# One layer of a hybrid encoder: the pieces of the folded down-projection weights move from SyncE's queue to ScalarE's, and their subtractions are tied to VectorE's order

## The chip, the cores and the metric

The kernel runs on 1 core of one Trainium2 chip. The metric is the device time of one execution in microseconds (us). Three executions of the kernel before took 2810.12, 2808.11 and 2813.13 us (median 2810.12).

## What is computed

One layer is applied to a prompt of 2048 rows and to 8 short sequences of 16 rows, all of width 1024:

```python
h = rms_norm(x, norm_g[0])
z = h @ w_in                      # columns split among attention heads and memory heads
att = band_attention(...)         # 8 heads x 64, own chunk and 8 chunks before, relative bias
mem = mlstm_sequence(...)         # 4 heads x 128, a recurrent matrix memory
x = x + rms_norm(concat(rms_norm(att), sigmoid(o) * head_norm(mem)) @ w_out, norm_g[1])
u = rms_norm(x, norm_g[2]) @ w_up # 1024 x 5632
y = causal_conv_width_3(u); gate, up = split(y)
x = x + rms_norm((gelu(gate) * up) @ w_down, norm_g[3])   # w_down: 2816 x 1024
```

Keys, values, memory states and convolution tails are outputs too.

## The kernel before

All matmuls run in fp32 pieces: each operand is split into a high part (a ScalarE cast or copy) and a low part (a VectorE subtraction), and `mm3` (L99 to L103) issues three matmuls per product.

The program has two large stages. In the first, rows are normed and multiplied by `w_in` in 14 column groups for each half of the rows (`seq`, 28 groups in all). While TensorE does those projections, two streams are interleaved with them by `pump`: band attention (lines 334 to 450) and the matrix memory (lines 500 to 800). The output projection by `w_out` follows. In the second stage, `w_up`, the convolution and `w_down` run in three row blocks. For the first two blocks, the products are done by a scheme of seven multiplications instead of eight, which needs sums and differences of blocks of the weights.

The differences of `w_down` are made ahead of time, in the first stage, by `folds` (L1163 to L1190). A row group of `w_down` holds four 128 x 512 blocks; `folds` handles 11 row groups in two halves each, 22 pieces. For a piece:

- `load` fetches 512 KB, 128 partitions by 4 by 256 numbers, into a buffer `fold` (three buffers take turns, L1173 and L1174);
- `combine` makes four subtractions in place on VectorE (L1179);
- `store` writes the 512 KB to the DRAM tensor `wtd` (L1183).

The second stage reads `wtd` (L1381) from 1732 us on. `folds` is a generator that is advanced one step per projection unit in the groups 2 to 12 of each half (the loop over `seq`). Piece i is fetched at step 12 i, combined nine steps later, stored fourteen steps after its fetch (`FOLD_STEPS = 12`, lags 0, 9 and 14).

What stands where on each engine is decided by a scheduler that reorders the recorded instructions by its own estimate of when inputs are ready. `tc.keep_in_program_order` takes an instruction out of that freedom in one direction: it may not stand ahead of the instruction that was recorded just before it on the same engine. Before the change the fetches and stores of the pieces are so tied, to SyncE's order; the subtractions are free. SyncE (SP) issues nearly all other DMAs: `wi_raw` (the raw `w_in` pieces, L1207), `qraw`, `kraw`, `vraw` (attention operands, L343 to L360), `mb` (memory operands, L673), `mvo`, `skr`, `svr`. ScalarE (ACT) issues 268 DMAs of its own, all stores of projection results (`qTd`, `kTd`, `qkbd` at L248, `vd`, `vobd` at L284). Its other work in this stage is the casts to high parts (`wi_h` L1213, `kh`, `svh`, `pth` L414), the copies of projection results out of PSUM (`qk_st`, `va_st`, `vo_st`, L233 and L235) and exponentials.

An engine's queue is served in order: behind an instruction that waits, all that follows on that engine waits too.

Of the kernel before, what the change touches and what calls it, by code (L numbers as in the profile page):

```python
# [13 lines left out]
ALU = mybir.AluOpType  # L14
# [36 lines left out]
def hymba_step(ctx: ExitStack, tc: tile.TileContext, I: dict, O: dict):  # L51
    nc = tc.nc
# [16 lines left out]
    def dt_(shape, name):  # L69
        return dram.tile(shape, F32, tag=name, name=name)  # L70
# [4 lines left out]
    def bcast(ap, shape):  # L75
        return ap.broadcast_to(shape)

    ident = const.tile([P, P], F32, name="ident")
    make_identity(nc, ident)
    nhalf = const.tile([P, 8], F32, name="nhalf")  # L80
# [41 lines left out]
    wtd = [dt_([P, 2048], f"wtd{k}") for k in range(NK)]  # L122
# [1042 lines left out]
    def folds():  # L1165

        v4 = lambda t: t.rearrange("p (a n) -> p a n", a=4)
        pieces = [(k, c) for k in range(NK) for c in range(2)]
        live = {}

        def load(i):
            k, c = pieces[i]
            live[i] = v4(pr.tile([P, D], F32, tag="fold", name=f"fold{k}_{c}", bufs=3))  # L1173
            tc.keep_in_program_order(nc.sync.dma_start(live[i], v4(I["w_down"][k])[:, :, c * 256:(c + 1) * 256]))  # L1174

        def combine(i):
            a, b, c, d = [live[i][:, x] for x in range(4)]
            for o, x, y in ((a, b, a), (b, c, b), (c, c, a), (d, d, c)):
                nc.vector.tensor_tensor(o, x, y, op=ALU.subtract)  # L1179

        def store(i):
            k, c = pieces[i]
            tc.keep_in_program_order(nc.sync.dma_start(v4(wtd[k])[:, :, c * 256:(c + 1) * 256], live.pop(i)))  # L1183

        for n in range(FOLD_STEPS * (len(pieces) + 2)):
            for lag, do in ((0, load), (9, combine), (14, store)):
                i, r = divmod(n - lag, FOLD_STEPS)
                if r == 0 and 0 <= i < len(pieces):
                    do(i)
            yield  # L1190
# [49 lines left out]
    for n_, (half, gi) in enumerate(seq):  # L1240
# [6 lines left out]
        i = int(g[2])  # L1247
# [226 lines left out]
    for b, tiles in enumerate(FBLOCKS):  # L1474
# [204 lines left out]
        if fast:  # L1679
# [47 lines left out]
            for p, (_, _, set_, onto) in enumerate(SEQUENCE):  # L1727
                for c in range(3):
# [8 lines left out]
                    for k in range(4 * c, min(4 * c + 4, NK)):  # L1737
                        i = 6 * p + k // 2
# [189 lines left out]
```

## Time and profile before

| what | value |
|---|---|
| profiled execution, its own time | 2809.85 us |
| span, first to last instruction | 2808.1 us |
| median of three executions | 2810.12 us |
| granted TensorE clock, mean | 0.990 |
| VectorE subtractions of the pieces | 88, 75.7 to 880.4 us |
| fetches and stores of the pieces | 22 and 22, 68.5 to 931.5 us |
| DMA traffic | 535.11 MB, mean 191 GB/s |

The profile's engines are PE (TensorE's matmuls), DVE (VectorE), ACT (ScalarE), POOL (GpSimd) and SP (SyncE). A q behind an engine's name marks its sequencer, which issues DMAs and waits for semaphores. Busy time leaves DMA issues out. In lists of waits, a row gives who waited for what, the sum in us, how many times, and the longest. In stretches of the timeline a row starts with its time in us from the span's start and its duration; brackets hold the idle time of the engine just before it and what ended that.

### The profile page before, as it was taken

The page shows a single profiled execution, that of the slowest core. Times are in us where ns is not written, and L with a number is a line of the kernel's source. Part 1 is how long each engine was busy: PE and PEld are TensorE (multiplying, and loading weights), DVE is VectorE, ACT ScalarE, POOL GpSimd, SP SyncE. Part 2 cuts the span into 40 slices and gives each one's busy share as a digit, 9 for nine tenths or more (in the row PEclk, how much of TensorE's full clock was granted, in tenths as well). Part 3 has the DMA queues.
Part 4 walks back from the last instruction along what each step waited for, and adds up shares of the span by engine and source line. Part 5 has one row for each costly group of instructions (what it writes and reads, how often), then busy time and mean ns, then how long its engine had stood idle before and what let it go on. Part 6 is the DMA issues. An engine that isn't in the chain of part 4 may idle for free.

```text
span 2808.1 us, 47256 instructions
## 1 busy us (share of the span) xinstructions
PE 2705.9 (96%) x16393; PEld 2529.3 (90%) x16393; DVE 1888.4 (67%) x3443; ACT 1518.6 (54%) x3164; POOL 451.9 (16%) x895
## 2 busy tenths in 40 slices
PE   8899999989999999999899999999999999999998
PEld 7899999988899997878899997889999778999887
DVE  5355556646556567767798888757777875777755
ACT  4354555634446666543455557656565656666533
POOL 1000010211100002234212111011111221222220
PEclk9999999999999999999999999999999999999999
DMA  5645456567675555445665557675555887555585
GB/s 183 175 130 168 147 169 207 161 182 228 197 214 148 157 159 181 130 144 185 214 197 185 173 178 267 198 237 173 175 174 163 293 284 236 176 179 174 180 314 188
DMA packets 359887, 535.11 MB, mean 191 GB/s; under 512 B 58882, under 2 KB 198110, under 8 KB 359518
## 3 DMA queue, kind: packets, MB, share of 16 engines
q1 hardware_dynamic: 319134, 491.95, 55.8%
q10 hardware_dynamic: 38592, 33.83, 3.6%
q0 software_dynamic: 1920, 6.29, 0.6%
q8 instruction: 129, 2.11, 0.3%
q14 instruction: 112, 0.92, 0.1%
HBM read 383.87 MB, written 151.21 MB: 191 GB/s over the span
## 4 chain that ended last, share of the span: by engine, by line
PE 68%; DMA 14%; DVE 9%; issue 4%; ACT 3%; POOL 1%; SPq 1%; DVEq 0%; ACTq 0%; POOLq 0%
PE udc L101 5%; PE udc L102 5%; PE udc L103 5%; PE dn L103 3%; PE dn L102 3%; PE dn L101 3%; PE ua L102 3%; PE ua L101 3%; PE ua L103 2%; DMA wu<-in_w_up 2%; PE dnm L103 2%; PE pt L73 2%; PE dnm L102 2%; PE dnm L101 2%; PE qb L101 2%
## 5 line engine op out<-in xcount | busy, mean ns | idle before, releaser
L101 PE MATMUL udc<-B,wuh 128*128 128x384 f32 (+1 forms) x720 | 236.6, 329 | 7.0 <-DVE uu L1641 7.0
L102 PE MATMUL udc<-B,wuh 128*128 128x384 f32 (+1 forms) x720 | 235.9, 328 | 0.0
L103 PE MATMUL udc<-B,wul 128*128 128x384 f32 (+1 forms) x720 | 235.6, 328 | 0.0
L1310 DVE TENSOR_TENSOR wul<-wu,wuh 128x512 fp32r<-128x512 f32 x255 | 165.1, 687 | 39.2 <-ACT wuh L1309 33.2
L1309 ACT CAST wuh<-wu 128x512 fp32r<-128x512 f32 x255 | 144.7, 622 | 53.6 <-PE udc L102 48.2
L101 PE MATMUL vo<-wi_h,hT 128*128 128x256 f32 x544 | 156.2, 287 | 0.7 <-ACT vo_st L233 0.7
L102 PE MATMUL vo<-wi_l,hT 128*128 128x256 f32 x544 | 155.7, 286 | 0.0
L103 PE MATMUL vo<-wi_h,hT 128*128 128x256 f32 x544 | 155.0, 285 | 0.0
L101 PEld LDWEIGHTS udc<-B,wuh 128*128 128x128 f32 x720 | 135.9, 189 | 9.1 <-DVE uu L1641 8.9
L1310 DVE TENSOR_TENSOR wdl<-wdr,wdh 128x512 fp32r<-128x512 f32 x198 | 129.1, 699 | 18.6 <-ACT wdh L1309 18.4
L102 PEld LDWEIGHTS udc<-B,wuh 128*128 128x128 f32 x720 | 135.8, 189 | 0.2
L101 PE MATMUL qk<-hT,wi_h 128*128 128x384 f32 (+1 forms) x384 | 129.7, 338 | 6.4 <-ACT qk_st L235 4.0
L103 PEld LDWEIGHTS udc<-B,wul 128*128 128x128 f32 x720 | 135.7, 189 | 0.0
L403 ACT ACTIVATE tmp<-tmp,mn 128x640 f32<-128x640 f32 (+4 forms) x128 | 97.6, 763 | 69.5 <-DVE mn L402 67.9
L1309 ACT CAST wdh<-wdr 128x512 fp32r<-128x512 f32 x198 | 112.7, 617 | 34.9 <-DMA wdr<-in_w_down 10.7
L402 DVE CUSTOM_DVE_ANT_0 tmp<-s,nb 128x640 f32<-128x640 f32 (+4 forms) x128 | 94.2, 736 | 52.7 <-PE s L392 52.0
L102 PE MATMUL dn<-wdl,ah 128*128 128x512 f32 x308 | 123.4, 401 | 5.7 <-DVE wdl L1310 5.7
L101 PE MATMUL qb<-hT,wi_h 128*128 128x384 f32 (+1 forms) x384 | 126.9, 331 | 1.7 <-ACT qk_st L233 1.7
L103 PE MATMUL qk<-hT,wi_l 128*128 128x384 f32 (+1 forms) x384 | 128.0, 333 | 0.0
L102 PE MATMUL qk<-hT,wi_h 128*128 128x384 f32 (+1 forms) x384 | 127.8, 333 | 0.0
L103 PE MATMUL qb<-hT,wi_l 128*128 128x384 f32 (+1 forms) x384 | 127.2, 331 | 0.0
L415 DVE TENSOR_TENSOR ptl<-pt,pth 128x640 fp32r<-128x640 f32 (+4 forms) x128 | 93.5, 737 | 49.8 <-ACT pth L414 49.0
(447 smaller groups left out, 9130.9 us busy)
## 6 DMA issues: line engine op xcount, KB each, us to landing
wu<-in_w_up SPq DMA_DIRECT2D x220, 256.0 KB, 3.8
wu<-wsd SPq DMA_DIRECT2D x176, 256.0 KB, 4.0
wdr<-in_w_down SPq DMA_DIRECT2D x110, 256.0 KB, 5.3
wi_raw<-in_w_in SPq DMA_DIRECT2D x52, 512.0 KB, 4.9
wsd<-ws SPq DMA_DIRECT2D x88, 256.0 KB, 2.8
wdr<-wtd SPq DMA_DIRECT2D x88, 256.0 KB, 6.3
ad_S<-g SPq DMA_DIRECT2D x88, 192.0 KB, 3.3
ar<-ad_S SPq DMA_DIRECT2D x40, 384.0 KB, 4.7
```

The costliest lines, as they stand in the source:

```text
L73: nc.tensor.transpose(out, in_, ident[:n, :n])
L101: nc.tensor.matmul(out, ah, bh, start=start, stop=False, skip_group_check=onto)
L102: nc.tensor.matmul(out, ah, bl, start=False, stop=False, skip_group_check=onto)
L103: nc.tensor.matmul(out, al, bh, start=False, stop=stop, skip_group_check=onto)
L402: nc.vector.tensor_tensor_reduce(o_, s_, b_, 1.0, 3e38, ALU.add, ALU.min, accum_out=mn)
L403: nc.scalar.activation(tmp[:, :n], tmp[:, :n], AF.Exp, bias=mn, scale=-1.0, accum_out=rsum[:, i % 4, hh:hh + 1])
L415: nc.vector.tensor_tensor(s.ptl[:, sl, qc], ptv, s.pth[:, sl, qc], op=ALU.subtract)
L1309: nc.scalar.copy(h, r)
L1310: nc.vector.tensor_tensor(l, r, h, op=ALU.subtract)
```

## The change

The three edits stand in `folds`. Fetch and store go to ScalarE's queue, each tied behind the ScalarE instruction recorded before it, and each subtraction is tied behind the VectorE instruction recorded before it. An added line gives the tying function a short name, so the line numbers behind it grow by one (L1174, L1179 and L1183 become L1175, L1180 and L1184).

```diff
+    pin = tc.keep_in_program_order
...
-            tc.keep_in_program_order(nc.sync.dma_start(live[i], v4(I["w_down"][k])[:, :, c * 256:(c + 1) * 256]))
+            pin(nc.scalar.dma_start(live[i], v4(I["w_down"][k])[:, :, c * 256:(c + 1) * 256]))
...
             for o, x, y in ((a, b, a), (b, c, b), (c, c, a), (d, d, c)):
-                nc.vector.tensor_tensor(o, x, y, op=ALU.subtract)
+                pin(nc.vector.tensor_tensor(o, x, y, op=ALU.subtract))
...
-            tc.keep_in_program_order(nc.sync.dma_start(v4(wtd[k])[:, :, c * 256:(c + 1) * 256], live.pop(i)))
+            pin(nc.scalar.dma_start(v4(wtd[k])[:, :, c * 256:(c + 1) * 256], live.pop(i)))
```

The scheduler lays out the whole first stage anew, on all engines; from the first matmuls of the second stage on, the order is the same but for some twenty rows late in its second row block. Three places matter for what follows.

The first is VectorE at the first piece, `fold0_0`, some 70 us into the program; `pks`, `cm` and `bp` belong to the memory stream. Before:

```order
L626 TENSOR_TENSOR pks_905<-as_876,cms_899 4x128
L1179 TENSOR_TENSOR fold0_0_1163<-fold0_0_1163 128x256 x2
L551 COPY colss_961<-pkTs_959 128x128
L1179 TENSOR_TENSOR fold0_0_1163<-fold0_0_1163 128x256
L543 COPY bp0_1042<-bap0_1038 32x128
L544 COPY ap0_1043<-bap0_1038 32x128
L1179 TENSOR_TENSOR fold0_0_1163<-fold0_0_1163 128x256
L563 SCALAR_TENSOR_TENSOR cm0_1046<-ap0_1043 32x128
```

With the change, VectorE reaches this piece here (`kl` and `tmp` are attention's, the fetch stands on ScalarE behind `pk`, at what was 94 us before):

```order
L587 TENSOR_TENSOR bp0_1042<-bp0_1042,cm0_1046 32x128
L1215 TENSOR_TENSOR wi3_l3_1147<-wi3_raw1_1228,wi3_h3_1146 128x512 x2
L353 TENSOR_TENSOR qs1_0_1349<-qraw1_0_1317,qs1_0_1349 64x512
L1180 TENSOR_TENSOR fold0_0_1163<-fold0_0_1163 128x256
L357 TENSOR_TENSOR kl1_0_1348<-kraw1_0_0_1318,kh1_0_1347 128x512
L552 COPY colsp_1138<-pkTp_1136 128x128
L403 ISA tmp0_0_1343,mn0_0_1344<-s0_0_1339,nb0_0_1242 128x128
L403 ISA mn0_0_1344 128x1
L403 ISA tmp0_1_1376,mn0_1_1377<-s0_1_1373,nb0_0_1242 128x256
L403 ISA mn0_1_1377 128x1
L1180 TENSOR_TENSOR fold0_0_1163<-fold0_0_1163 128x256 x3
```

The piece has moved back by about 20 us of VectorE's work, and its fetch has moved from 68 us to about 94 us.

The second place is ScalarE around 384 us: `num`, `jk`, `w` and `kw` are the memory stream's, `qb2` is a projection, `sph` attention's. Before:

```order
L712 ACTIVATE num0_0_4231<-ma0_0_1_4279,colsp_1138 128x129
L651 ACTIVATE jk0_0_1_4324,mssq0_0_4319<-num0_0_4231 128x128
L698 ACTIVATE w0_2_1_4372<-mb0_2_4151,colsp_1138 128x128
L233 COPY qb2_0_st0_2_5535<-qb2_0_0_2_5438 128x384
L248 DMA qkbd2_1_133<-qb2_0_st0_2_5535 128x256
L248 DMA qkbd2_4_136<-qb2_0_st0_2_5535 128x128
L899 CAST sph0_3919<-spt0_3913 128x512
```

With the change:

```order
L1184 DMA wtd3_243<-fold3_0_3739 512x1x256
L713 ACTIVATE num0_0_4231<-ma0_0_1_4279,colsp_1138 128x129
L234 COPY qb2_0_st0_2_5535<-qb2_0_0_2_5438 128x384
L249 DMA qkbd2_1_133<-qb2_0_st0_2_5535 128x256
L652 ACTIVATE jk0_0_1_4324,mssq0_0_4319<-num0_0_4231 128x128
L249 DMA qkbd2_4_136<-qb2_0_st0_2_5535 128x128
L699 ACTIVATE w0_2_1_4372<-mb0_2_4151,colsp_1138 128x128
L1175 DMA fold4_1_5018<-in_w_down 128x4x256
L900 CAST sph0_3919<-spt0_3913 128x512
```

Here a store is followed, six instructions later, by the fetch that reuses the stored buffer. Nine rows further on stands that piece's own store, and four rows behind it the fetch of `fold5_0` into the same buffer.

The third place is ScalarE around 577 us. Before, the two stores of `qk0_1_st0_1` are followed by `qk0_1_st0_2`, the next copy out of PSUM. With the change:

```order
L236 ACTIVATE qk0_1_st0_1_7627<-qk0_1_0_1_7555 128x384
L249 DMA qTd0_2_96<-qk0_1_st0_1_7627 128x128
L249 DMA qTd0_3_97<-qk0_1_st0_1_7627 128x256
L1184 DMA wtd5_245<-fold5_1_5987 512x1x256
L236 ACTIVATE qk0_1_st0_2_7683<-qk0_1_0_2_7631 128x256
```

A piece's store has come between them; on VectorE its four subtractions now stand behind `vz1_3`, which started at 581.70 us before.

## Prediction

> **What bounds the kernel now.** I read the busy table of the page first, then the busy time by stretch, then the waits of each engine in the stretch where the pieces are made, then the timeline at the longest of those waits. The first line is the page's busy table, the four behind it are stretches (stretch, its length, busy us and instructions of PE, PEld, DVE, ACT and POOL, granted clock, DMA share, GB/s).
>
> ```profile
> PE 2705.9 (96%) x16393; PEld 2529.3 (90%) x16393; DVE 1888.4 (67%) x3443; ACT 1518.6 (54%) x3164; POOL 451.9 (16%) x895
> ...
> 0.00:60.00 60.00, 46.51 (x335) 44.77 (x336) 33.60 (x65) 28.80 (x50) 9.63 (x33) 1.00 0.53 173
> 60.00:960.00 900.00, 863.98 (x6093) 836.54 (x6092) 492.57 (x1241) 437.92 (x1058) 72.06 (x224) 0.99 0.59 178
> 960.00:1360.00 400.00, 386.28 (x2334) 341.35 (x2332) 272.23 (x494) 213.12 (x513) 112.06 (x167) 0.99 0.52 167
> 1360.00:2808.10 1448.10, 1409.16 (x7637) 1306.62 (x7636) 1090.02 (x1645) 838.80 (x1545) 258.15 (x472) 0.99 0.64 206
> ```
>
> TensorE is the bound. All pieces are made between 60 and 960 us, and there TensorE is busy 863.98 of 900 us, so **36.0 us of idle time is all that a better order can win** in that stretch, with no matmul removed. The clock is 0.99 there and at full speed or nearly in all stretches, so nothing is to be had from it.
>
> What the change goes after stands in the waits of VectorE in this stretch and in the chain of waits cut to it (shares of 900 us). The two rows of issues are the page's: KB each and median us from issue to landing.
>
> ```profile
> DVE tmp L402 <- PE s L392: 50.3, 32, 4.0
> DVE wi_l L1214 <- ACT wi_h L1213: 49.1, 28, 4.3
> DVE fold L1179 <- DMA fold<-in_w_down: 43.3, 17, 9.4
> ...
> by line: DMA fold<-in_w_down 5.3%; PE qb L101 4.6%; PE qb L102 4.5%; PE qb L103 4.5%; issue 4.4%; PE pt L73 4.0%; PE vo L102 4.0%; PE vo L103 4.0%; PE vo L101 3.9%; DMA wi_raw<-in_w_in 3.4%; DMA mvo<-vobd 2.8%; PE qk L101 2.7%; PE qk L102 2
> ...
> fold<-in_w_down SPq DMA_DIRECT2D x22, 512.0 KB, 4.9
> wtd<-fold SPq DMA_DIRECT2D x22, 512.0 KB, 4.8
> ```
>
> VectorE stands 43.3 us, 17 times, before a subtraction whose piece has not landed. The chain names the fetch for 5.3%, 47.7 us. That is more than TensorE's whole idle time here, so the chain's share is no gain: it runs through waits that TensorE's queue of ready matmuls covered. What counts is which idle times of TensorE follow a piece's wait. The two longest waits and one later one, from the timelines of DVE, ACT, SP and PE:
>
> ```profile
> 75.72 0.89 DVE L1179 TENSOR_TENSOR fold<-fold 128x256 f32<-128x256 f32 x2 [7.07 <-DMA fold<-in_w_down]
> 79.76 0.18 PE L73 MATMUL rt<-ident,cm 32*1 32x32 f32 x1 [1.00 <-DVE cm L563]
> 85.53 0.17 PE L73 MATMUL mp<-ident,mrow 1*32 1x1 f32 x1 [0.95 <-DVE mrow L572]
> 93.49 0.44 PE L101 MATMUL qk<-hT,wi_h 128*128 128x384 f32 x1 [2.18 <-ACT qk_st L235]
> ...
> 110.72 1.80 DVE L1179 TENSOR_TENSOR fold<-fold 128x256 f32<-128x256 f32 x4 [9.42 <-DMA fold<-in_w_down]
> 109.33 0.48 ACT L233 COPY qk_st<-qk 128x384 f32<-128x384 f32 x1 [7.68 <-DMA qTd<-qk_st]
> 116.96 0.69 ACT L698 ACTIVATE w<-mb,colsp 128x128 f32<-128x128 f32 x2 [7.16 <-POOL mb L682]
> 111.20 0.60 SPq L1183 DMA_DIRECT2D wtd<-fold  x1
> 111.90 6.17 SPq L673 DMA_DIRECT2D mb<-md  x3
> 109.86 0.45 PE L101 MATMUL qk<-hT,wi_h 128*128 128x384 f32 x1 [1.75 <-ACT qk_st L233]
> 118.07 0.39 PE L101 MATMUL va<-wi_h,hT 128*128 128x256 f32 x1 [3.55 <-ACT qk_st L233]
> ...
> 340.00 0.43 DVE L1179 TENSOR_TENSOR fold<-fold 128x256 f32<-128x256 f32 x1 [1.52 <-DMA nbs<-relrow]
> 339.93 0.39 PE L101 MATMUL vo<-wi_h,hT 128*128 128x256 f32 x1 [0.69 <-ACT vo_st L233]
> 341.87 0.77 PE L73 MATMUL pt<-ident,tmp 128*128 128x128 f32 x5 [0.72 <-DVE ptl L415]
> ```
>
> These idle times add up to 1.00 + 0.95 + 2.18 + 1.75 + 3.55 + 0.69 + 0.72 = **10.8 us**, a quarter of the 43.3. The clearest is 3.55: ACT's copy stood behind `w`, which waited for `mb`, which SP issued at 111.90 right behind a piece's store.
>
> **The change part by part.** Subtractions, bytes and transfers stay as they are: 88, and 22 of 512 KB each way. Three things move.
>
> First, VectorE's waits. In the new order nearly every piece is fetched 10 us or more ahead of its subtractions, by the times that their neighbours had before; a landing takes 4.9. Two pieces keep a wait. `fold0_0` is fetched at about 94 us and wanted at 96, where VectorE was idle up to this row in any case:
>
> ```profile
> 100.67 0.43 DVE L365 TENSOR_TENSOR vhl<-vraw,vhl 128x256 fp32r<-128x256 f32 x1 [3.70 <-ACT vhl L364]
> ```
>
> `fold4_1` is counted below. What goes from TensorE is between nothing and 10.8 us. I take the three that hang directly on a piece (3.55, 0.69 and 0.72) and half of the other 5.88: **7.9 us gained**.
>
> Second, the 44 issues. On SP one takes 0.58 us at the median, on ACT only a smaller transfer is to be seen:
>
> ```profile
> L1174 SPq DMA_DIRECT2D fold<-in_w_down x22: 545/580/659, 68.5 to 870.1; - x22
> L1183 SPq DMA_DIRECT2D wtd<-fold x22: 560/590/1329, 111.2 to 931.5; - x22
> L284 ACTq DMA_DIRECT2D vobd<-vo_st x68: 326/327/392, 261.1 to 1066.6; - x68
> ```
>
> The shape sets the issue, so I take SP's 0.585: 44 x 0.585 = 25.7 us that ACT's sequencer has to give (14.4 at ACT's own 0.327). ACT is busy 437.92 of 900 us, so half falls into idle time: 12.9 us late, between 0 and 25.7.
>
> For SP the same 25.7 us go, and with them the waits of the pieces in SP's queue:
>
> ```profile
> SPq L1174 <- DMA wtd<-fold: 6.9, 2, 4.5
> SPq L449 <- DVE fold L1179: 6.1, 1, 6.1
> ```
>
> I cost this relief at nothing, since most loads there are issued ahead of need; at most it is 13.0 us at the quarter above, 3 us gained. The Trainium skill (DMA: Bandwidth & Descriptors, section Issuing engines are not separate DMA queues) speaks against more: transfers started on several engines run on the same 16 DMA engines, and only issue time is saved. By that the fetches land no sooner and the relief is the issues alone; if it did not hold, the 3 us would be nearer. No row here tells it apart.
>
> Third, ACT waits. A fetch into a buffer waits for the landing of that buffer's store, a store for the last subtraction. The rows of before at the three places where that falls badly:
>
> ```profile
> 385.83 0.46 ACT L233 COPY qb_st<-qb 128x384 f32<-128x384 f32 x1
> 387.48 0.59 ACT L899 CAST sph<-spt 128x512 fp32r<-128x512 f32 x1 [1.19 <-PE ma L709]
> 388.71 0.34 DVE L710 SCALAR_TENSOR_TENSOR cst<-cst,dec,ma 128x129 f32<-128x129 f32 x1
> ...
> 577.39 0.81 ACTq L248 DMA_DIRECT2D qTd<-qk_st  x2
> 581.76 0.39 ACT L235 ACTIVATE qk_st<-qk 128x256 f32<-128x256 f32 x1 [4.39 <-PE qk L103]
> 581.70 0.42 DVE L785 TENSOR_TENSOR vz<-mvos,ind 128x258 f32<-128x258 f32 x1
> ...
> 723.81 0.45 ACTq L248 DMA_DIRECT2D out_k_prompt<-qk_st  x1
> 727.56 1.13 ACT L1213 CAST wi_h<-wi_raw 128x512 fp32r<-128x512 f32 x2
> 731.97 0.42 DVE L785 TENSOR_TENSOR vz<-mvos,ind 128x258 f32<-128x258 f32 x1
> ```
>
> - At 384: the store of `fold3_0` goes at about 384.4 and lands 4.8 later, at 389.2; the fetch of `fold4_1` behind it would be reached at 386.4, and ACT stands 2.8 us. The piece lands at about 394.7, VectorE wants it at 389 and stands 5.5; four subtractions of 0.42 later ACT may store (397), and the fetch of `fold5_0` into the same buffer waits until 402, where ACT would have been at 394. ACT is 8 us late; the casts of `sph`, the memory stream's `kw` and `num` and the copies of `qb` are behind it.
> - At 577: ACT reaches the store of `fold5_1` at 577.8; its subtractions stand behind `vz`, 581.70, and end at 583.8. The copy that started at 581.76 comes 2.7 us later with the issue.
> - At 724: the store of `fold6_1` stands ahead of the casts of 727.56. Three of its subtractions follow `vz` of 731.97. If the memory stream keeps its old pace, ACT is 10 us late; in the new order its rows stand among attention rows that ran some 10 us earlier, and the wait then shrinks to 1 or 2. I take 5.
>
> The other stores are reached within 2 us of their subtractions' old places or well behind them: 3 us in all. ACT is late by 8 + 2.7 + 5 + 3 = 18.7 us, and by 12.9 from the issues: 31.6. How much of it TensorE feels no row shows; the nearest rate is the quarter above, 10.8 of 43.3: **7.9 us lost**, with ends at 0 and at all of it.
>
> Sum: 2809.85 - 7.9 + 7.9 = **2810 us**. The span is 2808.1, and 1.75 lie around it; the profiled execution stands 0.3 under the median of three, which changes nothing here.
>
> **The rivals.**
>
> VectorE's waits go and ACT's lateness stays covered: ACT idles half of the stretch, and of VectorE's 43.3 us three quarters never reached TensorE. 10.8 gained, 3 from SP, 1 lost at `fold0_0`: 2797. Against it: ACT's copies empty PSUM for TensorE, and 8.2 of the 10.8 us shown are waits for ACT.
>
> The chain is right, and more than the shown idle goes with the fetch: at the very most 36.0, 2774. Against it: 25 of the 36 us follow no wait for a piece.
>
> **ACT in order is worse than SP in order**: a store or a fetch that waits holds up copies and casts that TensorE needs at once, where on SP it held up loads. Lateness passes to TensorE once it exceeds ACT's lead over TensorE's wants, 4.39 us at 581.76. The three places would then cost 8 + 2.7 + 10 = 20.7 whole, and the issues 3.2 at the quarter: 2809.85 - 7.9 + 23.9 = 2826. For it: one landing of `qTd` that ACT waited for idled it 7.68 us before 109.33, and TensorE 1.75. Here the Trainium skill has a sentence (DMA: Bandwidth & Descriptors, section Anatomy of one DMA): DMA engines do not wait on semaphores; the wait is on the issuing sequencer, before dispatch. The row at 109.33 agrees.
>
> The change does not do what it says: the tie only sets a place behind one recorded instruction, and VectorE goes on waiting for pieces as at `fold4_1`. Then gain and loss are both small: 2811.
>
> **How the numbers follow.** A measurement of this kernel can tell about 0.2%, 5.6 us, from no change. Forecast, 2810 (its own range 2804.5 to 2815.5): 0.31. The change without effect: 0.05. Covered gain, 2797: 0.27. The whole idle: 0.03. ACT in order, 2826: 0.34. So faster 0.30, same 0.36, slower 0.34. The range from 2796 to 2828 leaves out the whole idle, the outer part of the slow rival (all 31.6 us passed on) and little else. The new order of the whole stage, which shifts attention and memory against the projections by up to some 10 us, can move idle times by a few us either way; the range holds that.
>
> **What would show it.** Right: VectorE's row of `fold` waits falls from 43.3 to some 10; idle time before 120 us on TensorE shrinks; ACT's queue gets rows that wait for `wtd` and for `fold` subtractions, some 20 us; TensorE's busy time in the stretch stays at 864. Wrong: ACT's waits of that kind over 35 us, with TensorE's idle time behind `qk_st`, `qb_st` or `wi_h` grown by more than 10 us (slow rival), or no such waits and idle under 26 us (gain).

## The result and the profile after

| what | before | after |
|---|---|---|
| median, 20 executions of each | 2809.12 us | 2811.82 us (2804.49 to 2819.93) |
| ratio, with its 95% interval | | 1.0004 [0.9994, 1.0013] |
| span of the profiled execution | 2808.1 us | 2806.2 us |
| granted TensorE clock, mean | 0.990 | 0.990 |

No change, as forecast (2810, "same"). (Ratios, here and below, leave out executions that took far longer than the others. Here the quotient of the two means, 2811.60 and 2810.50 us, is 1.0004 and that of the medians 1.0010; single executions of the changed kernel spread over 15 us.) Whether the two terms of 7.9 us that cancelled in the forecast exist is another question, and most of what follows is about it.

The page's busy table and the same stretches as before (busy us and instructions of PE, PEld, DVE, ACT and POOL, granted clock, DMA share, GB/s):

```profile
PE 2705.7 (96%) x16393; PEld 2529.0 (90%) x16393; DVE 1890.5 (67%) x3443; ACT 1521.3 (54%) x3164; POOL 445.7 (16%) x895
```

```profile
60.00:960.00 900.00, 867.01 (x6131) 842.31 (x6130) 493.01 (x1242) 441.26 (x1058) 71.61 (x224) 0.99 0.59 178
960.00:1360.00 400.00, 382.06 (x2299) 335.81 (x2297) 273.44 (x496) 214.00 (x512) 112.64 (x167) 0.99 0.52 167
1360.00:2806.20 1446.20, 1409.93 (x7636) 1305.53 (x7636) 1091.01 (x1644) 837.20 (x1545) 251.72 (x472) 0.99 0.63 206
```

Take TensorE's busy time from each stretch's length. From 60 to 960 us it idled 33.0 us (before 36.0), from 960 to 1360 it idled 17.9 (before 13.7), behind that 36.3 (before 38.9). So 3.0 us were won where the pieces are made, and 4.2 were given back in the next 400 us, where the stage ends. The span is 1.9 us shorter.

VectorE's longest waits from 60 to 960 us (who waited for what: us, times, longest):

```profile
DVE wi_l L1215 <- ACT wi_h L1214: 61.6, 34, 4.5
DVE ptl L416 <- ACT pth L415: 58.6, 46, 13.5
DVE tmp L403 <- PE s L393: 54.6, 40, 4.3
...
DVE attT L435 <- ACT sh L434: 26.3, 15, 4.2
```

Two rows of before that the prediction did not need stand against the second and the fourth:

```profile
DVE ptl L415 <- ACT pth L414: 39.4, 37, 6.3
...
DVE attT L434 <- ACT sh L433: 20.0, 13, 4.2
```

The rows of one tile, `fold`: duration of one in ns (min/median/max), first and last start, who it kept waiting, and the landing of its DMAs:

```profile
L1180 DVE TENSOR_TENSOR fold<-fold x88: 373/420/427, 96.1 to 922.9; 128x256 f32<-128x256 f32 x88
L1175 ACTq DMA_DIRECT2D fold<-in_w_down x22: 547/592/657, 90.5 to 870.9; - x22
L1184 ACTq DMA_DIRECT2D wtd<-fold x22: 530/574/616, 116.4 to 923.4; - x22
...
  DVE fold L1180: 2.8, 1
...
DMA to landing us min/median/max: 3.3/4.5/6.1
```

The row for pieces has fallen from 43.3 us, 17 times, to 2.8, once. VectorE's busy time has not moved (492.57 to 493.01), and its other waits have grown: for `pth` from 39.4 to 58.6, for `wi_h` from 49.1 to 61.6, for `sh` from 20.0 to 26.3, for `s` from 50.3 to 54.6. These four rows together grew by 42.3 us, 1.8 more than the piece's row lost. VectorE stands as long as before (its busy time in the stretch says so), under other names.

### The profile page after: what moved, and what is told of

Read it like the earlier page. It is cut to its first block, busy times and chain, and to the rows that moved or that the text cites. A ratio compares the mean times of both kernels' runs of the same rounds, so it can differ in the third digit from the quotient of the medians.

```text
span 2806.2 us, 47300 instructions
## 1 busy us (share of the span) xinstructions
PE 2705.7 (96%) x16393; PEld 2529.0 (90%) x16393; DVE 1890.5 (67%) x3443; ACT 1521.3 (54%) x3164; POOL 445.7 (16%) x895
## 4 chain that ended last, share of the span: by engine, by line
PE 41%; DVE 5%; DMA 5%; issue 2%; ACT 2%; SPq 0%; POOL 0%; DVEq 0%; POOLq 0%; ACTq 0%
PE udc L102 5%; PE udc L103 5%; PE udc L104 5%; PE dn L104 3%; PE dn L103 3%; PE dn L102 3%; PE ua L103 2%; PE ua L102 2%; PE ua L104 2%; DMA wu<-in_w_up 2%; PE dnm L104 2%; PE dnm L103 2%; PE dnm L102 2%; DMA ad_A<-g 1%; PE ue L104 1%
## 5 line engine op out<-in xcount | busy, mean ns | idle before, releaser
L102 PEld LDWEIGHTS udc<-B,wuh 128*128 128x128 f32 x720 | 135.7, 189 | 10.8 <-DVE uu L1642 7.9
L1310 ACT CAST wdh<-wdr 128x512 fp32r<-128x512 f32 x198 | 112.4, 618 | 36.7 <-DMA wdr<-in_w_down 13.7
```

Source lines behind the costliest of these rows:

```text
L102: nc.tensor.matmul(out, ah, bh, start=start, stop=False, skip_group_check=onto)
L1310: nc.scalar.copy(h, r)
```

## The experiments

Three theories were set against each other.

- **A, cancelling**, the forecast: VectorE's waits for pieces cost TensorE about 8 us before, and ScalarE's lateness costs about as much after.
- **B, covered**: neither reaches TensorE by more than 2 us.
- **C, layout**: every new order of the first stage moves TensorE's idle time by a few us, whatever is moved.

### The queue alone and the tie alone

The change has two halves. The first kernel keeps the pieces on ScalarE and leaves the subtractions free:

```diff
-                pin(nc.vector.tensor_tensor(o, x, y, op=ALU.subtract))
+                nc.vector.tensor_tensor(o, x, y, op=ALU.subtract)
```

> Fetches and stores on ScalarE's queue, subtractions free as before. Theory A (cancelling: VectorE's waits for pieces cost TensorE some 8 us before, ScalarE's lateness costs about as much with the change): VectorE's waits for pieces stay near 40 us, the cost on ScalarE is paid, so 2814 to 2820, ratio 1.002 to 1.004. Theory B (covered: neither reaches TensorE by more than 2 us): ratio 0.999 to 1.001. Theory C (each new layout of the stage moves TensorE's idle time by a few us, whatever the cause): anywhere within 0.998 to 1.003, with the difference in stretches that have nothing to do with pieces.

The second ties the subtractions and leaves the pieces on SP:

```diff
-            pin(nc.scalar.dma_start(live[i], v4(I["w_down"][k])[:, :, c * 256:(c + 1) * 256]))
+            pin(nc.sync.dma_start(live[i], v4(I["w_down"][k])[:, :, c * 256:(c + 1) * 256]))
...
-            pin(nc.scalar.dma_start(v4(wtd[k])[:, :, c * 256:(c + 1) * 256], live.pop(i)))
+            pin(nc.sync.dma_start(v4(wtd[k])[:, :, c * 256:(c + 1) * 256], live.pop(i)))
```

> Fetches and stores stay on SyncE's queue, subtractions tied. Theory A: VectorE's waits for pieces fall below 15 us and nothing is paid on ScalarE, so 2800 to 2804, ratio 0.997 to 0.998. Theory B: waits fall all the same, ratio 0.999 to 1.001. Theory C: within 0.998 to 1.003.

Measured: the queue alone 0.9998 [0.9986, 1.0011], the tie alone 1.0018 [1.0004, 1.0032], slower by 5 us. VectorE's waits for pieces from 60 to 960 us, first with the queue alone:

```profile
DVE fold L1180 <- DMA fold<-in_w_down: 43.4, 17, 6.3
```

then with the tie alone:

```profile
DVE fold L1180 <- DMA fold<-in_w_down: 6.9, 4, 2.7
```

It is the tie that takes the waits away; the queue has no part in it. Theory A gave the tie alone a gain and the queue alone a loss. The kernel that kept all 43.4 us of waits and took on ScalarE's issues is as fast as before, where A expected 1.002 to 1.004. The one that got rid of the waits at no cost to ScalarE is no faster but slower, where A expected 0.997 to 0.998. That goes against both terms of A. B (0.999 to 1.001) takes the first kernel; the 1.0018 of the second lies outside it, though the interval reaches down into it. C takes both.

### What the pieces cost in all

The next question was how much there is to win. This kernel makes no pieces: fetches, subtractions and stores are left out, and the second stage reads `w_down`'s own blocks in their place.

```diff
-            for lag, do in ((0, load), (9, combine), (14, store)):
+            for lag, do in ():
...
-            src = I["w_down"][k] if blk < 4 else wtd[k]
+            src = I["w_down"][k]
```

> Leaves out all 22 fetches, 88 subtractions and 22 stores; the second stage reads the weights' own blocks in place of the differences, the same number of bytes. Theory A: at least the 8 us of waits go, and 37 us of VectorE's work and 22 MB of traffic with them: 2795 to 2802, ratio 0.995 to 0.9975. Theory B: TensorE's idle time between 60 and 960 us belongs to other chains, it stays at 30 us or more, and the ratio is 0.998 to 1.000. This run is the most that any placing of the pieces could win.

Measured: 2780.89 us, 0.9904 [0.9891, 0.9916], 27 us less. The stretch where they would be made:

```profile
60.00:960.00 900.00, 878.54 (x6261) 853.57 (x6261) 473.65 (x1182) 449.67 (x1084) 75.61 (x230) 0.99 0.52 155
```

TensorE's idle time from 60 to 960 us is 21.5 us in place of 36.0. So the pieces do cost something, three times either term of A, and more than either theory expected: A had 0.995 to 0.9975, B 0.998 to 1.000 with 30 us of idle time or more. The change keeps every fetch, subtraction and store. Not all of the 27 us is idle time of TensorE: in the profiled executions the span is 25.7 us shorter, of which 19.4 are idle time and 6.3 busy time, 2699.6 in place of 2705.9 us for the same 16393 matmuls, at a granted clock of 0.993 in place of 0.990. Why the clock differs was not looked into.

### More issues, on ScalarE and on SP

If issuing is what costs, four times the issues should show it. Each fetch and each store is cut into four of 128 KB, 176 issues in place of 44, with the subtractions tied as in the change. On ScalarE (the store alike):

```diff
-            pin(nc.scalar.dma_start(live[i], v4(I["w_down"][k])[:, :, c * 256:(c + 1) * 256]))
+            for x in range(4):
+                pin(nc.scalar.dma_start(live[i][:, x], v4(I["w_down"][k])[:, x, c * 256:(c + 1) * 256]))
```

> As the change, with each fetch and each store cut into four of 128 KB: 176 issues on ScalarE in place of 44, the same bytes. At 0.33 us each that is 58 us of issue in place of 26. Theory A: 32 us more of issue, half of it late, a quarter of that on TensorE: 4 us or more over the change, 2815 to 2822. Theory B: within 2 us of the change, ratio to before 0.999 to 1.001.

The same on SP, with `nc.sync` for `nc.scalar`:

> Subtractions tied, each fetch and store cut into four of 128 KB as in the run with four issues on ScalarE, but all 176 on SyncE's queue. Theory A (issue time on ScalarE reaches TensorE, on SyncE it does not): close to the run with the tie alone, 2812 to 2818, and below the four issues on ScalarE (2818.5). Rival (any added issue delays the loads or casts that TensorE needs, whichever queue it is on): at or above the four issues on ScalarE, 2818 or more.

Measured: on ScalarE 1.0036 [1.0023, 1.0049], on SP 1.0064 [1.0052, 1.0076]. The issues on ScalarE:

```profile
L1176 ACTq DMA_DIRECT2D fold<-in_w_down x88: 334/443/1272, 89.4 to 881.2; - x88
...
L1187 ACTq DMA_DIRECT2D wtd<-fold x88: 326/350/1052, 115.7 to 928.8; - x88
```

By the medians, ScalarE now gives 88 x 0.443 + 88 x 0.350 = 69.8 us to the pieces' issues, where the changed kernel gives 22 x 0.592 + 22 x 0.574 = 25.7. These 44 us more go with about 9 us of time (0.0032 of 2810), a fifth. Taken alone, this run is what A expected (2815 to 2822 us; the median is 2818.51), and B's 0.999 to 1.001 missed. But on SP the same cut went with 13 us over the tie alone, where A expected it to be free; the rival there, by which added issues delay something on whichever queue they stand, had 2818 us or more, and 2826.92 came. The fear of the slow rival, that ScalarE in order is worse than SP in order, is not borne out: four times the issues did no more harm on ScalarE than on SP. Nor does the harm on SP lie where the issues stand: from 60 to 960 us TensorE idles 36.3 us (before 36.0), and 13.2 of its 14.0 us of added idle time come behind 960 us, when the last piece has been stored. (How much of the 8 us between the two is the queue, and how much the layout, is a question for the last experiment.)

### The pieces from GpSimd's queue

GpSimd is busy 72 of the 900 us, so ScalarE could be spared altogether. The changed kernel with `nc.gpsimd` for `nc.scalar` in both lines:

> As the change, but fetches and stores from GpSimd's queue. GpSimd is busy 16%, and what waits behind a piece there is the norms' small steps and the memory stream's scales. Theory A: neither ScalarE nor SyncE pays the 26 us of issue, so below the change and below before by 3 us or more, 2800 to 2806. Rival (issue time is not what the pieces cost): within 3 us of before, 2805 to 2812.

Measured: 1.0055 [1.0043, 1.0068], 15 us slower; A's expectation and its rival's both missed. The rows of `fold`:

```profile
L1175 POOL DMA_DIRECT2D fold<-in_w_down x22: 751/806/959, 2.1 to 913.5; - x22
L1184 POOL DMA_DIRECT2D wtd<-fold x22: 713/758/793, 99.9 to 939.2; - x22
...
  DVE fold L1180: 95.6, 6
...
DMA to landing us min/median/max: 3.4/6.0/9.4
```

The third row is GpSimd, which stood 95.6 us before stores that waited for subtractions; behind them in its queue are the masks and selects of the memory stream. An issue took 0.76 to 0.81 us, and a landing 6.0 at the median against 4.5. Which of the three made the 15 us was not taken apart.

### Transfers alone and subtractions alone

The kernel before without the 88 subtractions (what is stored is then the weights themselves):

```diff
-            for lag, do in ((0, load), (9, combine), (14, store)):
+            for lag, do in ((0, load), (14, store)):
```

> Before without the 88 subtractions: a fetched piece is stored as it came. Without any piece the time fell by 27 us. If the transfers cost it (issue on SyncE, 22 MB of traffic, loads that land later): 2800 to 2808. If VectorE's work and its waits for pieces cost it: 2781 to 2788. Half and half would be 2794.

The kernel before with the 88 subtractions on three buffers that were set to zero, without a fetch or a store; the second stage reads `w_down`'s own blocks:

```diff
-            a, b, c, d = [live[i][:, x] for x in range(4)]
+            a, b, c, d = [v4(still[i % 3])[:, x] for x in range(4)]
...
-            for lag, do in ((0, load), (9, combine), (14, store)):
+            for lag, do in ((9, combine),):
```

> Before with the 88 subtractions made on three buffers that stay in place, no fetch and no store; the second stage reads the weights' own blocks. 37 us of VectorE's work without a wait for a transfer. If VectorE's work costs the 27 us: 2798 to 2806. If the transfers, or the waits for them, cost it: 2781 to 2788.

Measured: transfers alone 0.9958 [0.9942, 0.9974], subtractions alone 0.9938 [0.9925, 0.995]. Both lie between the ranges that were expected. The second cannot be read as it was meant. Its subtractions wait for nothing but the setting to zero, and the scheduler put all 88 at the very start of the program:

```profile
L1182 DVE TENSOR_TENSOR still<-still x88: 404/415/531, 2.6 to 65.6; 128x256 f32<-128x256 f32 x88
```

There TensorE is busy 41.90 of the first 60 us, where it is busy 46.83 without pieces, and behind 66 us no subtraction is left. So this run does not say what the subtractions cost where the kernel makes them. What remains is the kernel with transfers alone: against the kernel without pieces (0.9904) its transfers cost 0.0054 or 15 us, and the other 12 of the 27 us go to the subtractions and to the waits for pieces together, which these two kernels do not tell apart. (By the medians the two kernels of this section lie 16.6 and 12.5 us above the one without pieces, and an expectation further on takes the 12.5 for the price of the subtractions.) That reading leans on differences of a few thousandths, each between two layouts.

### Transfers alone, on ScalarE

The changed kernel with the same edit, so that fetches and stores run from ScalarE and no subtraction is there to wait for:

> The changed kernel without the 88 subtractions: the 22 fetches and 22 stores, issued on ACT, stay (the output is not the reference's; what is stored is the weights themselves). Its pair is the same with the pieces on SP, which took 0.9958 of the kernel before. Theory B (the queue that issues the pieces costs nothing either way): 0.995 to 0.997, 2795 to 2801 us. Theory A (ACT late by 25.7 us of issues and by waits, passed on at a quarter, 6 us or more, now without any relief for VectorE): 0.998 or above, 2803 us or more. Theory C: anywhere within 5 us of its pair.

Measured: 0.9947 [0.9929, 0.9964], where its pair on SP had 0.9958 [0.9942, 0.9974]. The intervals overlap: no sign that the transfers cost more from ScalarE's queue than from SP's, and A's 0.998 or above missed (B's 0.995 to 0.997 by a little, on the other side).

The two kernels with transfers alone also allow a comparison on the waits. To leave out the subtractions won 0.0042 or 12 us where VectorE had stood 43.3 us before them (the kernel before), and 0.0057 or 16 us where it had stood 2.8 (the change). If those waits had a price, the first should have won more. Each of these differences, too, is one between two layouts.

### The subtractions on GpSimd

This takes both the waits and the work off VectorE:

```diff
-                nc.vector.tensor_tensor(o, x, y, op=ALU.subtract)
+                nc.gpsimd.tensor_tensor(o, x, y, op=ALU.subtract)
```

> The kernel before with the 88 subtractions on GpSimd in place of VectorE, everything else as it was. Without the subtractions (and with the transfers) the kernel took 0.9958, and the subtractions alone cost 12.5 us over none. If what they cost is VectorE's time (theory B: waits and queues are free, work is not), GpSimd, which is idle for over 800 of the 900 us, takes them for little: 0.995 to 0.997, 2795 to 2801 us, with 55 to 90 us more of busy time on GpSimd and VectorE's rows of fold gone. If it is the waits for the pieces (theory A), GpSimd now stands them ahead of the masks and selects that the memory stream waits for: 0.999 to 1.003. Theory C: the whole stage is laid out anew, 5 us to either side of that.

Measured: 1.0001 [0.999, 1.0012]. The stretch, and GpSimd's row of waits for pieces:

```profile
60.00:960.00 900.00, 866.04 (x6103) 839.74 (x6102) 468.60 (x1152) 437.03 (x1055) 141.39 (x312) 0.99 0.59 178
```

```profile
POOL fold L1179 <- DMA fold<-in_w_down: 261.1, 21, 40.7
```

VectorE has no wait for a piece left and 24 us less work in the stretch, GpSimd stands 261.1 us for pieces, and the time is the same. B's expectation of 0.995 to 0.997 missed. A's of 0.999 to 1.003, by which GpSimd's waits for pieces would now hold up the memory stream's masks, was met in its number. So VectorE's 43.3 us of waits and 37 us of subtractions (88 x 0.42) went and nothing was won, but that does not show that they had no price: GpSimd's waits and its slower subtractions came in their place, and no run separates the two. Some of the price was paid in another coin: of the 37 us only 24 left VectorE. With GpSimd subtracting, rows of VectorE that ran beside it took longer. Here are both engines near 575 us, in the memory stream's small rows (start us, us):

```profile
574.68 2.12 POOL L1179 TENSOR_TENSOR fold<-fold 128x256 f32<-128x256 f32 x3 [0.19 <-DMA fold<-in_w_down]
...
575.49 4.00 DVE L529 SCALAR_TENSOR_TENSOR lg_q_p<-lg_q_p,lg_s_p 128x32 f32<-128x32 f32 x7
...
577.13 2.31 POOL L1179 TENSOR_TENSOR fold<-fold 128x256 f32<-128x256 f32 x3
...
579.52 0.19 DVE L530 SCALAR_TENSOR_TENSOR lg_q_p<-lg_q_p,lg_s_p 128x32 f32<-128x32 f32 x1
```

The same seven rows of L529 took 0.19 us each in the kernel before, 1.3 in all in place of 4.00.

### The same kernel, laid out otherwise

The last two change nothing but where the pieces fall: one number of the kernel before, `FOLD_STEPS`, the spacing of the pieces, 11 and 13 in place of 12.

```diff
-FOLD_STEPS = 12
+FOLD_STEPS = 11
```

> The kernel before with pieces spaced 11 steps apart in place of 12: same work, same queues, another place for each piece. Theory C (each new layout of the stage moves the time by a few us, so that the 5 us by which the tie alone was slower say nothing about the tie): off 1 by 0.001 to 0.003 to either side, 2 to 8 us. Theories A and B: VectorE's waits and the queues are of the same size, so 0.999 to 1.001.

> The kernel before with pieces spaced 13 steps apart, which takes the last pieces later into the stage. Theory C: off 1 by 0.001 to 0.003 to either side, and not by the same amount as with 11. Theories A and B: 0.999 to 1.001.

Measured: spacing 11 gave 1.0031 [1.0016, 1.0046], spacing 13 gave 0.9970 [0.9958, 0.9982]. In us that is 8.7 more and 8.4 less, to either side of a kernel that does the same work from the same queues. A and B expected 0.999 to 1.001 for both and missed; C's "0.001 to 0.003 to either side" is what came, 0.0001 past its end with 11. The waits of VectorE and the stretch with 11:

```profile
DVE fold L1179 <- DMA fold<-in_w_down: 46.3, 17, 7.8
```

```profile
60.00:960.00 900.00, 857.82 (x6041) 828.24 (x6040) 487.97 (x1229) 433.25 (x1046) 75.69 (x224) 0.99 0.58 177
```

and with 13:

```profile
DVE fold L1179 <- DMA fold<-in_w_down: 48.9, 21, 10.6
```

```profile
60.00:960.00 900.00, 869.65 (x6154) 842.27 (x6153) 494.18 (x1246) 439.73 (x1062) 74.49 (x224) 0.99 0.59 177
```

TensorE idles 42.2 us in the one and 30.4 in the other, where before had 36.0. **The fastest kernel with all its pieces is the one in which VectorE waits longest for them**, 48.9 us. It beats both the kernel before and the changed one (2798.62 us median, beside 2807.60 of the kernel before on the same chip), and not because anything waits less.

All fourteen kernels in one table; the idle column is the page's span less TensorE's busy time, of one profiled execution each. It is not the whole of the time: TensorE's busy time goes from 2697.7 us (subtractions alone, at a granted clock of 0.994) to 2712.6 (four issues on SP, at 0.987), and with spacing 11 the profiled execution, 2807.51 us, was one of the fastest of a kernel with a median of 2816.00.

| kernel | pieces issued by | waits for pieces, us | TensorE idle, us | ratio to before |
|---|---|---|---|---|
| before | SP | 43.3 | 102.2 | 1 |
| after | ScalarE | 2.8 | 100.5 | 1.0004 |
| queue alone | ScalarE | 43.4 | 102.5 | 0.9998 |
| tie alone | SP | 6.9 | 101.8 | 1.0018 |
| subtractions on GpSimd | SP | 261.1, on GpSimd | 101.7 | 1.0001 |
| spacing 11 | SP | 46.3 | 104.1 | 1.0031 |
| spacing 13 | SP | 48.9 | 94.6 | 0.9970 |
| four issues each | ScalarE | 17.0 | 105.5 | 1.0036 |
| four issues each | SP | 3.2 | 116.2 | 1.0064 |
| pieces from GpSimd | GpSimd | 21.8 | 108.7 | 1.0055 |
| transfers alone | SP | none | 99.7 | 0.9958 |
| transfers alone | ScalarE | none | 91.8 | 0.9947 |
| subtractions alone | none | none | 95.8 | 0.9938 |
| no pieces | none | none | 82.8 | 0.9904 |

There is no order in the column of waits that the column of times follows.

## Why the prediction was right, and where its steps were wrong

The time and the verdict were right. Of the two terms, neither was borne out. That two terms which were not seen had been forecast at the same size, so that the sum came to 2810, is luck as far as these runs can tell.

**The bound** was right. TensorE is busy 2705.7 us after and 2705.9 before, so that between these two profiles only its idle time differs. In the stretch it is busy 867.01 where 864 was forecast.

**VectorE's waits** fell to 2.8 us at one place, forecast "some 10". The place was the one named, `fold4_1` near 384 us.

**"7.9 us gained" was not borne out.** The step took idle times of TensorE that stand near a piece's wait as caused by it. TensorE's idle time in the stretch fell by 3.0 us with the waits gone, and no kernel above that still makes all its pieces and got rid of VectorE's waits became faster than before. Two of the idle times that were counted as hanging directly on a piece, 0.69 and 0.72, do not hang on a wait for one: the row at 340.00 waited its 1.52 us for `nbs`, the 0.69 ended at 339.93, ahead of that row, and the 0.72 stands behind subtractions at work, not behind a wait for a piece. The early idle times that carried 9.4 of the 10.8 us show how the step went wrong. Here is the same place after, rows of ScalarE and TensorE between 75 and 121 us:

```profile
81.97 0.44 PE L102 MATMUL qk<-hT,wi_h 128*128 128x384 f32 x1 [1.88 <-ACT qk_st L234]
...
91.42 0.33 PE L73 MATMUL pkTp<-ident,pk 128*128 128x128 f32 x1 [0.50 <-ACT pk L589]
...
104.14 0.69 ACT L699 ACTIVATE w<-mb,colsp 128x128 f32<-128x128 f32 x2 [2.91 <-POOL mb L683]
...
105.25 0.69 PE L102 MATMUL qk<-hT,wi_h 128*128 128x384 f32 x1 [4.58 <-ACT qk_st L236]
```

Five early idle times of 9.4 us (1.00, 0.95, 2.18, 1.75 and 3.55) have become three of 7.0 (1.88, 0.50 and 4.58). The largest has grown by a microsecond, and it ends as before with a copy to `qk_st` that stands in ScalarE's queue behind `w`, which waits for `mb`. The forecast laid that wait to a piece's store on SP, right ahead of `mb`'s issue. But the store, by its row, took 0.60 us of SP's queue; ahead of both stood the four issues of `kraw`:

```profile
105.54 5.62 SPq L346 DMA_DIRECT2D kraw<-kTd  x4
```

With the change no store of a piece comes from SP any more; ScalarE's wait for `mb` is 2.91 us in place of 7.16, and the idle time of TensorE is longer, not shorter.

**"44 x 0.585 = 25.7 us"** was right as an issue price: 0.592 for a fetch and 0.574 for a store on ScalarE, so SP's price held and ScalarE's own 0.327 did not.

**"18.7 us" of waits on ScalarE was too large**, at two of the three places named. At 384, forecast 8 us late:

```profile
381.71 0.59 ACTq L1184 DMA_DIRECT2D wtd<-fold  x1
...
385.07 0.57 ACTq L1175 DMA_DIRECT2D fold<-in_w_down  x1
...
390.26 0.43 DVE L1180 TENSOR_TENSOR fold<-fold 128x256 f32<-128x256 f32 x1 [2.81 <-DMA fold<-in_w_down]
...
392.23 0.57 ACTq L1184 DMA_DIRECT2D wtd<-fold  x1
...
393.52 0.50 PE L102 MATMUL sot<-svh,sph 128*128 128x512 f32 x1 [0.23 <-ACT svh L911]
...
395.51 0.55 ACTq L1175 DMA_DIRECT2D fold<-in_w_down  x1
...
396.10 0.37 ACT L713 ACTIVATE num<-ma,colsp 128x129 f32<-128x129 f32 x1 [1.81 <-DMA wtd<-fold]
```

The chain is the one that was forecast, link by link: store, fetch, VectorE's wait (2.81, forecast 5.5), the store that waits for the subtractions, the fetch that waits for the store's landing. But each link came earlier. The first store left 2.7 us ahead of the forecast, the fetch followed it after 3.4 us and not 4.8 or more, and ScalarE stood 1.81 us at the end in place of 8. From 388 to 404 us TensorE has one idle time, the 0.23 quoted.

At 577 the forecast was 2.7 us, and it came:

```profile
581.65 0.81 ACTq L249 DMA_DIRECT2D qTd<-qk_st  x2
...
583.39 1.80 DVE L1180 TENSOR_TENSOR fold<-fold 128x256 f32<-128x256 f32 x4
...
585.22 0.59 ACTq L1184 DMA_DIRECT2D wtd<-fold  x1
...
585.91 0.38 ACT L236 ACTIVATE qk_st<-qk 128x256 f32<-128x256 f32 x1 [4.29 <-DMA qTd<-qk_st]
...
587.06 0.46 PE L696 MATMUL ms<-mqk 128*128 128x128 f32 x2 [1.22 <-DMA mqk<-qkbd]
```

ScalarE's sequencer had its last issue done at 582.46, the fourth subtraction ended at 585.19, and the store left at 585.22: 2.76 us. (The row at 585.91 names `qTd` for the 4.29 us; the times show the store ahead of it.) From 580 to 600 us TensorE has one idle time, the 1.22 of the last row, and that waits for `mqk`, not for this copy.

At 724 the forecast was 5 us, between 10 and "1 or 2":

```profile
720.93 0.50 ACTq L249 DMA_DIRECT2D out_k_prompt<-qk_st  x1
...
721.19 1.34 DVE L1180 TENSOR_TENSOR fold<-fold 128x256 f32<-128x256 f32 x3
...
722.10 2.27 ACTq L1184 DMA_DIRECT2D wtd<-fold  x2
...
724.41 0.74 ACT L890 ACTIVATE stmp<-stmp,smn 128x528 f32<-128x528 f32 x1 [4.42 <-DMA out_k_prompt<-qk_st]
```

The issue ahead of the two stores ended at 721.43, the first store left at 722.10, and of the 2.27 us of both some 1.1 are issuing: ScalarE stood about 1.8 us. (The 4.42 of the last row hold all this, the issues too.) It is the smaller of the two cases that the forecast weighed; the subtractions had come forward with the attention rows. The three places together came to some 6.4 us, where 15.7 were forecast.

**"7.9 us lost" was not borne out** either. It took a rate of a quarter, 10.8 of 43.3, from the step above, and put it on 31.6 us that were partly not there. The queue alone measured 0.9998, transfers alone no worse from ScalarE than from SP. The rule of the Trainium skill that was weighed there (DMA: Bandwidth & Descriptors, section Issuing engines are not separate DMA queues) agrees with the trace in this: away from SP's other loads, pieces landed 4.5 us after issue at the median against 4.8, hardly sooner.

**The rivals.** The covered gain has the queue alone and the transfers from ScalarE for it, in that no cost of ScalarE's lateness was seen; its 10.8 us of gain were not seen either. The slow rival's price of 2826 was not reached by the change; 1.0064 and 1.0055 were reached by more issues on SP and by GpSimd, not by ScalarE. The rival without effect had the right sum (2811), but not for its reason, since the tie did just what it says.

**The term that was missing** is the layout. The forecast had it as a closing remark, "idle times by a few us either way". Spacing alone moves the time by 8.7 us up and 8.4 down, as much as either term of the sum. Theory C is shown as far as this: one number changed, with work, queues and waits of about the same size, does that. It follows that no single pair of kernels here can pin a mechanism worth less than about 8 us. What remains of A and B is bounds: the change's halves and the kernel with GpSimd's subtractions lie between 0.9998 and 1.0018, so no effect of 7.9 us either way is seen in any of them. One of a few us is not excluded, nor is a larger one that a layout happened to hide.

**What stays open.** Why the tie alone is 5 us slower than before while the whole change is not is within the layout's spread, and was not taken apart. The 27 us that the pieces cost are shown as a whole, a part of them at a higher granted clock; how they split into transfers (15) and the rest (12) rests on differences close to that spread, and what the subtractions cost without their waits was not measured. Which of TensorE's idle times moved when the spacing changed was not followed row by row.

## What to carry to other kernels

An idle time that stands near a wait need not be caused by it: look whether another wait would have ended at the same moment, and take the next later one as the price that stays. Where a scheduler lays out a stage anew, first measure what a layout is worth by changing a number that should not matter (here a spacing: 0.3% either way), and treat it as a term with both signs; a forecast of a smaller term is a forecast of noise. And before ordering the waits of a side task, measure the kernel without the task: here it was worth 1%, and its waits nothing that stood out from the layouts. When a kernel is built to measure one part alone, look in its trace where that part ended up: here 88 subtractions without a wait ran to the start of the program.

## What the runs showed of the hardware

- Issuing a 512 KB DMA of this shape took as long on ScalarE (0.57 to 0.59 us at the median) as on SP (0.58 to 0.59), and 0.76 to 0.81 on GpSimd. Cut into four, a part took 0.35 to 0.44 at the median on ScalarE, so that the cut raised the sum 2.7 times.
- A subtraction of 128 x 256 numbers takes 0.42 us on VectorE, and on GpSimd:

```profile
L1179 POOL TENSOR_TENSOR fold<-fold x88: 723/739/1892, 76.7 to 876.2; 128x256 f32<-128x256 f32 x88
```

While GpSimd subtracted, rows of VectorE stretched. L529 of the same kernel goes up to 674 ns:

```profile
L529 DVE SCALAR_TENSOR_TENSOR lg_q_p<-lg_q_p,lg_s_p x14: 183/194/674, 64.9 to 578.9; 128x32 f32<-128x32 f32 x14
```

where the kernel before has 185 to 193 for all fourteen:

```profile
L529 DVE SCALAR_TENSOR_TENSOR lg_q_p<-lg_q_p,lg_s_p x14: 185/191/193, 64.6 to 580.0; 128x32 f32<-128x32 f32 x14
```

Work put into GpSimd's idle time was thus not free of charge to VectorE here.
